# Square sums on TensorE, a new order of need in the first stage, and weights asked for ahead of the queries, in a two-layer diffusion backbone

## The chip, the cores and the metric

The kernel runs on 1 core of one Trainium2 chip. The metric is device time in microseconds (us) for one execution; lower is better. Given is the median of several runs. The engines are named as the profile names them: PE is TensorE (matmul) and PEld its weight load, DVE is VectorE, ACT is ScalarE, POOL is GpSimd, SP is SyncE, whose queue issues nearly all DMA transfers.

## The reference

A backbone of two layers runs over 1280 tokens of width 1024: 256 context tokens and 1024 latent ones. A layer normalizes its input, modulates it by a vector from the conditioning, mixes the tokens and adds the result back through a gate.

```
def rms_norm(x, g):
    y = x * lax.rsqrt(jnp.mean(x * x, axis=-1, keepdims=True) + EPS)
    return y * g
def modulation(cond, w, b):
    return jnp.split(jax.nn.silu(cond) @ w + b, 3, axis=-1)
for i in range(DEPTH):                                  # DEPTH = 2
    sh_l, sc_l, g_l = modulation(c, mod_w[i], mod_b[i])
    sh_c, sc_c, g_c = modulation(c_ctx, mod_w[i], mod_b[i])
    h_lat = rms_norm(x_lat, norm_g[i]) * (1.0 + sc_l) + sh_l
    h_ctx = rms_norm(x_ctx, norm_g[i]) * (1.0 + sc_c) + sh_c
    if i % 2 == 0: y_lat, y_ctx = even_mixer(h_lat, h_ctx, ...)
    else:          y_lat, y_ctx = odd_mixer(h_lat, h_ctx, ...)
    x_lat = x_lat + g_l * y_lat
    if i < DEPTH - 1: x_ctx = x_ctx + g_c * y_ctx
return rms_norm(x_lat, final_g)
```

Layer 0 (even) has two kinds of grouped attention, a global one with rotary and normalized queries and keys, and a banded one with a sink logit. Layer 1 (odd) has a gated convolution over 31 tokens and a neighbourhood attention on the grid. The projections in front of each are one large matmul of `h`.

## The kernel before, in words

The 1280 tokens are kept transposed, with the width on the partitions: 8 tiles of 128 (index `dk`, constant `DK`). Tokens go in three chunks: chunk 0 is the context (256 tokens), chunks 1 and 2 are 512 latent tokens each. All is fp32. A product of full accuracy is made of three matmuls (`mm3`, L344): each operand is split into a high part, rounded by an ACT cast (L325), and a rest, which POOL or DVE gets by subtraction (L328, or L339 in one step with the shift). So `hh`/`hl` are the two parts of a latent chunk's `h`, `hc` both parts of the context's, `wh`/`wl` those of weights.

A norm is made in steps. ACT squares the eight tiles; the squares are added up tile by tile (`acc`); a matmul with `ones` adds over the partitions (`trs`, L262, in `rstd_steps`); DVE scales it (`rbv`, L265); POOL raises it to -1/2 (L247) and three small DVE steps refine that (`nt`, `nt`, `nr`, L248 to L250); a matmul with the identity spreads it over the partitions (`bc`, L273). `make_h` (L330) then multiplies x by the gain and `bc` on DVE (L335, 8 instructions per chunk), and ACT adds the shift. There is also `sum4` (L276), in which four matmuls with 32 columns each add four tiles of squares into four quarters of one PSUM bank (L280). Before the change only the final norm uses it.

The first stage is written out by a string of events, `PLAN`: `p` constants, `0` `1` `2` load a chunk, `n` squares and adds (`norm_x`, L733), `b` `trs` to `bc` (`norm_bc`), `h` `make_h`, `m` a half of the modulation (a GEMV whose 32-column matmuls are `pm`, L183), `w` the first unit's weights. All three chunks go through it before `fill0(0, w0)` is run, which projects the first of four key/value units (`pq`: per block of 128 tokens, 8 x 3 matmuls of 384 columns; the transposes behind it are `trk`) and the first gate blocks (`pg`). Then comes the main loop: attention of one unit, woven with the projection of the next. `load_q` (L617, in `group0`) brings a block of queries from DRAM, over the SP queue.

The order in which each engine gets its instructions is not the order of the code: a scheduler simulates the program and sorts each engine's instructions by its own estimate, with priorities. `issue_after(ins)` pins an instruction behind `ins`, if both are on the same engine.

At the end of layer 0, `final_proj(c)` (L981) adds the output projection into x and makes the squares of layer 1's norm: for chunk 1, one ACT square per tile and seven adds (L1000), alternating between POOL and DVE. In the attention of that stretch, `QL` (L451) carries a running maximum into the scores, `st` are the scores, `ov` the sums over values, `mx` the matmuls for a maximum. In the tail, `final_norm` multiplies the output by `final_g` and `bc` on DVE (L1508) or POOL (L1498), block by block, with pins; the adds of the last block before it are L1440.

Of the kernel before, what the change touches and what calls it, by code (L numbers as in the profile page):

```python
# [10 lines left out]
F32 = mybir.dt.float32  # L11
F32R = mybir.dt.float32r
ALU = mybir.AluOpType
# [59 lines left out]
PLAN = 'p0mmnbwmm1h2nbhnbh'  # L73
MWR = "ABxAVx"
XA = 4
ORDER = (2, 3, 0, 1)
# [11 lines left out]
def tile_kernel(ctx: ExitStack, tc: tile.TileContext, a, out):  # L88
# [164 lines left out]
    last = []  # L253

    def rstd_steps(pool, accs, n, tag, inv=1.0, tr="tr"):
# [4 lines left out]
        for b in range(nb):  # L260
            for k, acc in enumerate(accs):
                last.append(PE.matmul(tr[:, 2 * b : 2 * b + 2], acc[:, b * P : (b + 1) * P], ones, start=(k == 0),  # L262
                                      stop=(k == len(accs) - 1)))
        v = pool.tile([P, 8], F32, tag="rbv", name=nm("rbv"), bufs=2)
        rv = VE.tensor_scalar(v[:, :nb], tr[:, 0 : 2 * nb].rearrange("p (b two) -> p b two", two=2)[:, :, 0],  # L265
                              inv, EPS, op0=ALU.mult, op1=ALU.add)
        r = newton_rsqrt(pool, v[:, :nb], nb, "rb")
# [4 lines left out]
        for b in range(nb):  # L272
            PE.matmul(bc[:, b * P : (b + 1) * P], r[:, b : b + 1].broadcast_to([P, P]), ident, start=True, stop=True)  # L273
# [41 lines left out]
    acts = []  # L315
# [14 lines left out]
    def make_h(l, c, xs, bc, h):  # L330

        cond = 1 if c == 0 else 0
        for dk in range(DK):
            x = xs(dk)
            VE.scalar_tensor_tensor(x, x, gs[l][:, dk, cond : cond + 1], bc, op0=ALU.mult, op1=ALU.mult)  # L335
# [4 lines left out]
            else:  # L340
                SC.activation(x, x, AF.Identity, bias=shift)
                split(x, h[0][:, dk, :], h[1][:, dk, :])

# [11 lines left out]
    def load_w(pool, src, blk, width, bufs, leng="g", dks=range(DK), rb=WPR):  # L355
# [4 lines left out]
        for d2 in sorted({dk // 2 for dk in dks}):  # L360
# [3 lines left out]
            SY.dma_start(raw[:, k], src[blk, d2, :, k])  # L364
# [249 lines left out]
    def group0(u, qb):  # L614
        isb = u >= 2

        def load_q(QH, QL):  # L617
            src = Qd[u][qb].rearrange("(e d) s a t -> d s e (a t)", e=2)
            for dst, s in ((QH[0:64, :], 0), (QH[64:128, :], 0), (QL[0:64, :], 1)):
                SY.dma_start(dst.bitcast(F32).rearrange("d (e c) -> d e c", e=2), src[:, s])  # L620
# [85 lines left out]
    with ExitStack() as p0x:  # L706
# [6 lines left out]
        with tc.tile_pool(name="st0", bufs=1, reuse_waits="tile") as st0:  # L713
# [19 lines left out]
            def norm_x(c):  # L733
                n = CHUNKS[c][1]
                acc = kvp.tile([P, 512], F32, tag="QH", name=nm("acc"), bufs=3)
                for dk in range(DK):
                    if dk == 0:
                        SC.activation(acc[:, :n], xraw[c][0], AF.Square)
                    else:
                        sq = kvp.tile([P, 512], F32, tag="QL", name=nm("sq"), bufs=3)  # L740
                        SC.activation(sq[:, :n], xraw[c][dk], AF.Square)
                        VE.tensor_tensor(acc[:, :n], acc[:, :n], sq[:, :n], op=ALU.add)
                return acc

            def norm_bc(c, acc):
                n = CHUNKS[c][1]
                return run(rstd_steps(st0, [acc], n, "st"))[:, :n]
# [920 lines left out]
```

## Time and profile before

| what | value |
|---|---|
| median of 3 runs | 1542.24 us (1541.05 to 1546.29) |
| profiled execution | 1542.41 us, its span 1540.6 us |
| granted TensorE clock, mean | 0.971 |
| TensorE busy | 95% of the span |
| VectorE, POOL, ScalarE busy | 68%, 51%, 48% |
| DMA | 199.83 MB, mean 130 GB/s |
| chain that ended last, by engine | PE 76%, DVE 12%, DMA 5%, issue 3% |

A row of the timeline has the start, the time, the engine, the line of the kernel, the operation and its tiles (output `<-` inputs), the shape and the count; in brackets stands how long the engine was idle before it, and what released it. A row of windows has the busy time of each engine in a stretch, and at its end the granted TensorE clock (1.00 is full speed), the DMA share and GB/s. Times in a timeline are of matmuls that overlap: how far apart they start says more than how long each takes.

### The profile page before, as it was taken

The numbers are of one execution on the slowest core, as the hardware profiler recorded it, in microseconds if no ns is written. First come the engines' busy times: TensorE is split into PE (matmuls) and PEld (weight loads), VectorE is DVE, ScalarE is ACT, GpSimd is POOL, SyncE is SP. The second block draws the span as 40 slices with busy tenths as digits, with TensorE's granted clock in tenths as the row PEclk, the third lists the DMA queues.
The fourth block names the chain that finished last, engine by engine and source line by source line (L and its number), as shares of the span: only waits on it lengthen the run. The fifth ranks groups of instructions, "written<-read, shape, count | busy, mean of one in ns | idle before, by whom it ended". The sixth has DMA issues, their size and how long they took to land.

```text
span 1540.6 us, 21500 instructions
## 1 busy us (share of the span) xinstructions
PE 1457.2 (95%) x7112; PEld 1171.6 (76%) x7112; DVE 1042.5 (68%) x2106; ACT 746.1 (48%) x1416; POOL 793.3 (51%) x631
## 2 busy tenths in 40 slices
PE   6899999998998999999999889999999999989996
PEld 2776888796896777886776558888887788868875
DVE  2833466479678956556667948999938675567866
ACT  3721434444444455447546665443434455455564
POOL 3440335446355757557646665665533434364664
PEclk7899999999999999999999889999999999999998
DMA  9474315423312236121111112211484677877642
GB/s 367 151 243 145 103 62 175 147 64 93 120 56 71 89 124 225 52 69 53 42 43 58 44 33 79 59 56 41 141 258 143 204 214 225 261 225 235 186 125 109
DMA packets 154168, 199.83 MB, mean 130 GB/s; under 512 B 14717, under 2 KB 95817, under 8 KB 154057
## 3 DMA queue, kind: packets, MB, share of 16 engines
q1 hardware_dynamic: 147392, 186.88, 38.6%
q10 hardware_dynamic: 6664, 11.57, 2.2%
q8 instruction: 56, 0.92, 0.3%
q14 instruction: 56, 0.45, 0.1%
HBM read 148.07 MB, written 49.02 MB: 128 GB/s over the span
## 4 chain that ended last, share of the span: by engine, by line
PE 76%; DVE 12%; DMA 5%; issue 3%; POOL 2%; ACT 2%; SPq 0%; DVEq 0%; POOLq 0%; ACTq 0%
PE p L345 6%; PE p L346 6%; PE p L347 6%; PE ov L473 4%; PE ov L475 4%; PE ov L474 4%; PE po L345 4%; PE po L347 4%; PE po L346 4%; PE st L522 4%; PE st L526 4%; PE pq L345 3%; PE pq L346 3%; PE pq L347 3%; PE pg L345 2%
## 5 line engine op out<-in xcount | busy, mean ns | idle before, releaser
L328 POOL TENSOR_TENSOR pl<-pf,ph 128x512 fp32r<-128x512 f32 (+4 forms) x321 | 395.3, 1243 | 369.2 <-ACT ph L325 305.8
L534 ACT ACTIVATE pf<-st 128x512 f32<-128x512 f32 x284 | 166.3, 597 | 199.3 <-PE st L526 160.8
L328 POOL TENSOR_TENSOR wl<-wr,wh 128x512 fp32r<-128x512 f32 (+2 forms) x131 | 171.0, 1317 | 145.9 <-ACT wh L325 131.5
L325 ACT CAST ph<-pf 128x512 fp32r<-128x512 f32 (+4 forms) x364 | 209.4, 588 | 28.2 <-PE ov L474 17.9
L345 PE MATMUL p<-hh,wh 128*128 128x512 f32 x448 | 176.2, 394 | 3.1 <-DVE spq L1166 1.4
L346 PE MATMUL p<-hl,wh 128*128 128x512 f32 x448 | 174.5, 390 | 0.0
L347 PE MATMUL p<-hh,wl 128*128 128x512 f32 x448 | 173.0, 391 | 0.0
L522 PE MATMUL st<-QH,KAt 128*128 128x512 f32 (+4 forms) x364 | 141.7, 390 | 6.9 <-ACT pf L534 6.0
L473 PE MATMUL ov<-ph,Vt 128*128 128x512 f32 (+4 forms) x364 | 140.8, 387 | 3.8 <-DVE y L683 2.0
L475 PE MATMUL ov<-pl,Vt 128*128 128x512 f32 (+4 forms) x364 | 141.0, 387 | 2.1 <-POOL pl L328 2.0
L474 PE MATMUL ov<-ph,Vt 128*64 128x512 f32 (+4 forms) x364 | 138.9, 382 | 0.0
L526 PE MATMUL st<-QL,KBt 68*128 68x512 f32 (+4 forms) x364 | 136.5, 386 | 0.9 <-issue 0.8
L325 ACT CAST wh<-wr 128x512 fp32r<-128x512 f32 (+2 forms) x134 | 81.0, 612 | 96.3 <-PE p L346 18.7
L1110 DVE SCALAR_TENSOR_TENSOR cps<-U,taps,cps 128x512 f32<-128x512 f32 x184 | 125.9, 749 | 0.7
L345 PEld LDWEIGHTS p<-hh,wh 128*128 128x128 f32 x448 | 84.2, 188 | 21.2 <-ACT wh L325 1.8
L347 PEld LDWEIGHTS p<-hh,wl 128*128 128x128 f32 x448 | 84.1, 188 | 17.5
L346 PEld LDWEIGHTS p<-hl,wh 128*128 128x128 f32 x448 | 84.2, 188 | 16.8 <-issue 0.2
L646 DVE TENSOR_REDUCE mp<-mx 128x1 f32<-128x512 f32 x128 | 85.2, 680 | 17.2 <-PE mx L645 16.3
L345 PE MATMUL pq<-wh,hh 128*128 128x384 f32 x256 | 88.0, 344 | 2.8 <-ACT hh L325 2.8
L967 DVE SCALAR_TENSOR_TENSOR x<-po,modT,x 128x512 f32<-128x512 f32 (+1 forms) x72 | 47.0, 657 | 63.2 <-PE po L347 62.8
L522 PEld LDWEIGHTS st<-QH,KAt 128*128 128x128 f32 x364 | 70.0, 193 | 24.4 <-ACT pf L534 9.1
L475 PEld LDWEIGHTS ov<-pl,Vt 128*128 128x128 f32 x364 | 70.1, 193 | 22.4 <-POOL pl L328 5.0
(283 smaller groups left out, 3473.8 us busy)
## 6 DMA issues: line engine op xcount, KB each, us to landing
mw<-in_mod_w_dram SPq DMA_DIRECT2D x16, 1024.0 KB, 5.5
Q<-qs SPq DMA_DIRECT2D x40, 256.0 KB, 2.2
QH<-Q SPq DMA_DIRECT2D x80, 128.0 KB, 2.7
mw<-in_mod_w_dram SPq DMA_DIRECT2D x16, 512.0 KB, 6.5
wr<-in_od_d_dram SPq DMA_DIRECT2D x32, 256.0 KB, 3.2
wr<-in_ev_qkv_dram SPq DMA_DIRECT2D x16, 384.0 KB, 5.2
KAt<-KD SPq DMA_DIRECT2D x16, 384.0 KB, 6.5
wr<-in_od_wo_dram SPq DMA_DIRECT2D x22, 256.0 KB, 3.4
```

The costliest lines, as they stand in the source:

```text
L325: acts.append(SC.copy(hi, src))
L328: (GP if leng == "g" else VE).tensor_tensor(lo, src, hi.bitcast(F32), op=ALU.subtract)
L345: PE.matmul(o, lh, rh, start=first, stop=False)
L346: PE.matmul(o, lh, rl, start=False, stop=False)
L347: last.append(PE.matmul(o, ll, rh, start=False, stop=end))
L473: PE.matmul(o, V[:, 64:192], ph[:, :n], start=(t == 0), stop=False)
L474: PE.matmul(g.ov[0:64, q0 : q0 + n], V[:, 0:64], ph[:, :n], start=False, stop=False)
L475: PE.matmul(o, V[:, 64:192], pl[:, :n], start=False, stop=(last and g.sink is None))
L522: sts.append(PE.matmul(st[:, :n], KA[:, cs], g.QH[:, q0 : q0 + n], start=True, stop=False))
L526: PE.matmul(st[:, :n], KB[0:68, cs], g.QL[0:68, q0 : q0 + n], start=False, stop=True)
L534: acts.append(SC.activation(pf[:, :n], st[:, :n], AF.Exp, scale=1.0 if g.bias else SCALE))
L1110: VE.scalar_tensor_tensor(pc, uc, w, pc, op0=ALU.mult, op1=ALU.add)
```

## The change

It has five parts.

1. *First stage.* Chunk 1's eight squares are kept, and two `sum4` groups on PE add them into one bank; ACT copies that to `acc`, and the scale 1/32 makes up for the 32 columns. The string has chunk 1's squares and norm ahead of chunk 0's `make_h`. Chunk 2's squares, norm and `make_h` leave the string: the new `start0` runs them at steps 6, 12 and 14 of the first unit's projection, with pins: the squares behind chunk 0's last cast and the copy, the adds behind chunk 1's last x multiply, `trs` behind the last recorded matmul. `BCP` pins two places of the first unit's `pq` (block 1 from dk = 6, block 5 from dk = 1) behind the last recorded `bc`.
2. *Second unit's weights.* They are asked for right behind the first unit's projection, and the first three query loads are pinned behind the last of these loads.
3. *End of layer 0.* `final_proj(1)` adds its squares by two `sum4` groups and one ACT copy in place of seven adds.
4. *Final pins.* In the first of the last blocks, DVE's multiply of tile 1 is pinned behind the last eight adds, and those of later tiles behind the root's third step. In the next block, POOL's multiply is pinned behind a DVE step (before: behind the POOL power).
5. The rest of the program is the same, but the scheduler re-times it.

```diff
-PLAN = 'p0mmnbwmm1h2nbhnbh'
+PLAN = 'p0mmnbwmm1nh2bh'
+S2 = (6, 12, 14)
+BCP = ((1, 6), (5, 1))
...
             def norm_x(c):
                 n = CHUNKS[c][1]
+                if c == 1:
+                    pb = bank("st", nm("pb"))
+                    for q in range(2):
+                        sqs = []
+                        for i in range(4):
...
+                            SC.activation(sq[:, :n], xraw[c][4 * q + i], AF.Square)
+                            sqs.append(sq)
+                        sum4(pb, sqs, n, q)
+                    acc = kvp.tile([P, 512], F32, tag="QH", name=nm("acc"), bufs=3)
+                    acts0.append(SC.copy(acc[:, :n], pb[:, :n]))
+                    return acc
...
-        for _ in fill0(0, w0):
-            pass
+        def start0(w):
+            for k, _ in enumerate(fill0(0, w)):
+                if k == S2[0]:
+                    acc = norm_x(2)
+                if k == S2[1]:
+                    b2 = rstd_steps(ap, [acc], 512, "st", pin=last[-1], vn=("ss", 16, "sr"))
+                    next(b2)
+                if k == S2[2]:
+                    with tc.issue_after(last[-1].ins):
+                        bc = run(b2)
+                    make_h(0, 2, lambda dk: xraw[2][dk], bc, h[2])
+
+        start0(w0)
+        w1 = load_w0("ev_qkv", ORDER[1])
+        firstq += 3 * dmas[-1:]
...
         def load_q(QH, QL):
+            with ExitStack() as cx:
+                if firstq:
+                    cx.enter_context(tc.issue_after(firstq.pop().ins))
...
-                weave(main, n1, fill0(k + 1), NFILL[k], False)
+                weave(main, n1, fill0(k + 1, w1 if k == 0 else None), NFILL[k], False)
...
-                if e < na:
+                if c == 1:
+                    sqs.append(op_.tile([P, 512], F32, tag="sq1" if e % 4 < 3 else "acc1", name=nm("sq1"), bufs=3 if e % 4 < 3 else 1))
+                    SC.activation(sqs[-1], x1[c][:, e, :], AF.Square)
+                    if e == 0:
+                        pb = bank("tr", nm("pb"))
+                    if e % 4 == 3:
+                        sum4(pb, sqs[-4:], n, e // 4)
+                    if e == 7:
+                        accs[c].append(acc1())
+                        SC.copy(accs[c][0], pb)
+                elif e < na:
...
                         if k == 1:
-                            cx.enter_context(tc.issue_after(roots[-1][1].ins))
+                            cx.enter_context(tc.issue_after(roots[-1][2].ins))
...
-                        if k == 0 and e > 1:
-                            pins = adds[-DK:] + ([roots[-2][2]] if e > 3 else [])
+                        if k == 0:
+                            pins = [roots[-2][2]] if e > 1 else adds[-DK:]
```

What it moves is shown at three places. The line numbers of the kernel after are up to some seventy higher; the numbers of tiles differ between the two.

The first place is PE in the first stage, where chunk 0's `pq` end. Before:

```order
L347 MATMUL pq_558<-wh_287,hc_171 128x384
L347 MATMUL pq_588<-wh_287,hc_171 128x384
L262 MATMUL trs_414<-ones,acc_391 128x2 x4
L262 MATMUL trs_483<-ones,acc_460 128x2 x4
L273 MATMUL bc_427<-ident,nr_421 128x128 x4
L345 MATMUL pq_629<-wh_269,hh_172 128x384
```

After (`trs_418` and `bc_431` are chunk 1's; `pq_564` is its first projection):

```order
L353 MATMUL pq_493<-wl_288,hc_171 128x384
L267 MATMUL trs_418<-ones,acc_372 128x2 x4
L354 MATMUL pq_493<-wh_287,hc_171 128x384
L278 MATMUL bc_431<-ident,nr_425 128x128 x4
L352 MATMUL pq_523<-wh_287,hc_171 128x384
L353 MATMUL pq_523<-wl_288,hc_171 128x384
L354 MATMUL pq_523<-wh_287,hc_171 128x384
L352 MATMUL pq_523<-wh_287,hc_171 128x384
L353 MATMUL pq_523<-wl_288,hc_171 128x384
L354 MATMUL pq_523<-wh_287,hc_171 128x384
L352 MATMUL pq_564<-wh_269,hh_172 128x384
```

Chunk 2's sums (`trs_483`) are no longer between chunk 1's sums and its `bc`; one `pq` of chunk 0 stands between them, and six stand behind `bc`. The two new groups of sums stand 21 matmuls and more ahead of this place, on PE after:

```order
L286 MATMUL pb_347<-sq_354,one 32x512
L286 MATMUL pb_347<-sq_348,one 32x512
L286 MATMUL pb_347<-sq_350,one 32x512
L286 MATMUL pb_347<-sq_352,one 32x512
L353 MATMUL pq_523<-wl_276,hc_171 128x384
L354 MATMUL pq_523<-wh_275,hc_171 128x384
L286 MATMUL pb_347<-sq_366,one 32x512
L286 MATMUL pb_347<-sq_360,one 32x512
L286 MATMUL pb_347<-sq_362,one 32x512
L286 MATMUL pb_347<-sq_364,one 32x512
```

Seventeen `pq` follow these rows up to chunk 1's `trs`.

The second place is PE later in the first unit's projection, where a part of the modulation (`pm`) goes. Before:

```order
L183 MATMUL pm_715<-mw_642,csil 32x512
L892 MATMUL trk_826<-ident,pc_628 128x128
L183 MATMUL pm_715<-mw_642,csil 32x512 x3
L183 MATMUL pm_715<-mw_644,csil 32x512 x2
L345 MATMUL pq_836<-wh_269,hh_174 128x384
L183 MATMUL pm_715<-mw_644,csil 32x512
L346 MATMUL pq_836<-wl_270,hh_174 128x384
L183 MATMUL pm_715<-mw_644,csil 32x512
```

After:

```order
L354 MATMUL pq_941<-wh_269,hl_175 128x384
L352 MATMUL pq_941<-wh_269,hh_174 128x384
L185 MATMUL pm_686<-mw_577,csil 32x512 x4
L185 MATMUL pm_686<-mw_579,csil 32x512 x4
```

The eight matmuls of this part stood in five pieces; now they are two whole groups in a row.

The third place is DVE at the end of layer 0. Before (`x_1776` is chunk 1's x, `QL_8450` belongs to an attention block):

```order
L429 TENSOR_REDUCE nmt_8534<-mp_8465 128x4
L248 TENSOR_TENSOR nt_9167<-nr_9166,rbv_9164 128x4
L249 SCALAR_TENSOR_TENSOR nt_9167<-nt_9167,nr_9166 128x4
L250 SCALAR_TENSOR_TENSOR nr_9166<-nt_9167,nr_9166 128x4
L328 TENSOR_TENSOR hc_7129<-y_8633,hc_7129 128x2x128
L328 TENSOR_TENSOR pl_8733<-pf_8734,ph_8732 128x512
L451 TENSOR_TENSOR QL_8450<-trn_8569,k_bd 4x512
L635 TENSOR_REDUCE mp_8639<-mx_8640 128x2
L335 SCALAR_TENSOR_TENSOR x_1776_7151<-x_1776_7151,gs_105,bc_9220 128x512 x8
```

After:

```order
L656 TENSOR_REDUCE mp_8469<-mx_8521 128x1
L656 TENSOR_REDUCE mp_8469<-mx_8535 128x1
L436 TENSOR_REDUCE nmt_8538<-mp_8469 128x4
L341 SCALAR_TENSOR_TENSOR x_1778_7155<-x_1778_7155,gs_105,bc_9228 128x512 x8
L458 TENSOR_TENSOR QL_8454<-trn_8573,k_bd 4x512
L645 TENSOR_REDUCE mp_8643<-mx_8644 128x2
```

The eight x multiplies of chunk 1's `make_h` stood behind this block's `QL`; now they stand ahead of it.

More of the change, by code (lines that the diff above doesn't have):

```diff
@@ L251, in newton_rsqrt, with rstd_steps @@
         return r
-    last = []
-    def rstd_steps(pool, accs, n, tag, inv=1.0, tr="tr"):
+    last, bcm = [], []
+    def rstd_steps(pool, accs, n, tag, inv=1.0, tr="tr", pin=None, vn=("rbv", 8, "rb")):
         nb = n // P
@@ L261, in rstd_steps @@
             for k, acc in enumerate(accs):
-                last.append(PE.matmul(tr[:, 2 * b : 2 * b + 2], acc[:, b * P : (b + 1) * P], ones, start=(k == 0),
-                                      stop=(k == len(accs) - 1)))
-        v = pool.tile([P, 8], F32, tag="rbv", name=nm("rbv"), bufs=2)
+                with ExitStack() as cx:
+                    if pin is not None:
+                        cx.enter_context(tc.issue_after(pin.ins))
+                    last.append(PE.matmul(tr[:, 2 * b : 2 * b + 2], acc[:, b * P : (b + 1) * P], ones, start=(k == 0),
+                                          stop=(k == len(accs) - 1)))
+        v = pool.tile([P, vn[1]], F32, tag=vn[0], name=nm("rbv"), bufs=2)
         rv = VE.tensor_scalar(v[:, :nb], tr[:, 0 : 2 * nb].rearrange("p (b two) -> p b two", two=2)[:, :, 0],
                               inv, EPS, op0=ALU.mult, op1=ALU.add)
-        r = newton_rsqrt(pool, v[:, :nb], nb, "rb")
+        r = newton_rsqrt(pool, v[:, :nb], nb, vn[2])
         roots.append((rv, *newt))
@@ L746, in norm_bc @@
                 n = CHUNKS[c][1]
-                return run(rstd_steps(st0, [acc], n, "st"))[:, :n]
+                return run(rstd_steps(st0, [acc], n, "st", 1.0 / 32.0 if c == 1 else 1.0))[:, :n]
             made = [0]
-            accs, bcs, mh = [], [], [(0, 0), (0, 1), (1, 0), (1, 1)]
+            sums, acts0, accs, bcs, mh = [], [], [], [], [(0, 0), (0, 1), (1, 0), (1, 1)]
             mwp[0] = st0
@@ L768, in tile_kernel @@
                 elif ev == "h":
-                    make_h(0, made[0], lambda dk, c=made[0]: xraw[c][dk], bcs[made[0]], h[made[0]])
+                    xg = make_h(0, made[0], lambda dk, c=made[0]: xraw[c][dk], bcs[made[0]], h[made[0]])
+                    if made[0] == 0:
+                        acts0.append(acts[-1])
+                    if made[0] == 1:
+                        sums.append(xg)
                     made[0] += 1
```

57 lines of the change are left out of this document (39 added, 18 removed).

## The prediction

> **What bounds the kernel now.** The first page and its slices of the span come first: TensorE is the engine that is nearly always busy, and the slices in which it is not are the first, the ones about 5/9 of the way, and the last. So I read three places: the start (to 110 us), the end of layer 0 (840 to 940) and the tail (from 1515).
>
> ```profile
> span 1540.6 us, 21500 instructions
> ...
> PE 1457.2 (95%) x7112; PEld 1171.6 (76%) x7112; DVE 1042.5 (68%) x2106; ACT 746.1 (48%) x1416; POOL 793.3 (51%) x631
> ```
>
> The profiled execution took 1542.41 us, 1.8 more than its span and 0.17 above the median of the three runs, 1542.24; I add to 1542.4. About 0.3%, 4.6 us, is what a measurement of this kernel can tell from no change.
>
> At the start TensorE's timeline shows this (pq is the projection of the first unit, trs the column sums of the squares, bc the broadcast of 1/rms; the last bracket is idle time and its releaser):
>
> ```profile
> 46.91 0.33 PE L347 MATMUL pq<-wh,hc 128*128 128x384 f32 x1
> 47.08 0.33 PE L345 MATMUL pq<-wh,hc 128*128 128x384 f32 x1
> ...
> 47.77 0.95 PE L262 MATMUL trs<-ones,acc 128*128 128x2 f32 x8
> 52.10 1.84 PE L262 MATMUL trs<-ones,acc 128*128 128x2 f32 x8 [3.38 <-DVE nt L249]
> 53.80 2.06 PE L273 MATMUL bc<-ident,nr 128*128 128x128 f32 x8
> 58.61 0.69 PE L345 MATMUL pq<-wh,hh 128*128 128x384 f32 x1 [2.76 <-ACT hh L325]
> ...
> 59.42 0.52 PE L345 MATMUL pq<-wh,hh 128*128 128x384 f32 x1
> 59.74 0.52 PE L346 MATMUL pq<-wl,hh 128*128 128x384 f32 x1
> ```
>
> TensorE runs out of chunk 0's pq at 47.8, does chunk 1's sums, and then stands for 3.38 us in front of chunk 2's sums, which are queued ahead of chunk 1's bc; bc is followed by another 2.76. What those sums wait for is on VectorE and GpSimd:
>
> ```profile
> 51.26 0.69 DVE L742 TENSOR_TENSOR acc<-acc,sq 128x512 f32<-128x512 f32 x1
> ...
> 55.26 0.16 DVE L248 TENSOR_TENSOR nt<-nr,rbv 128x4 f32<-128x4 f32 x1 [1.12 <-POOL nr L247]
> ...
> 55.89 5.36 DVE L335 SCALAR_TENSOR_TENSOR xr<-xr,gs,bc 128x512 f32<-128x512 f32 x8 [0.27 <-PE bc L273]
> ```
> ```profile
> 54.22 1.01 POOL L247 TENSOR_TENSOR nr<-rbv,mhalf 128x4 f32<-128x4 f32 x1 [3.12 <-DVE rbv L265]
> 58.64 3.81 POOL L328 TENSOR_TENSOR hl<-xr,hh 128x512 fp32r<-128x512 f32 x3 [3.41 <-ACT hh L325]
> ```
>
> VectorE adds squares one by one, 0.69 each, for both chunks, up to 51.9. The idle stretches also cost clock: pq starts 0.17 us apart at 47 and 0.32 apart at 59.
>
> **The change, part by part. (1) First chunk-1 projection.** Chunk 1's seven adds leave VectorE; two groups of four narrow matmuls enter TensorE. The same width stands in the modulation's pm, four of which (x8 in the records) run side by side:
>
> ```profile
> 86.45 1.04 PE L183 MATMUL pm<-mw,csil 128*32 128x512 f32 x2
> ...
> 87.69 1.90 PE L183 MATMUL pm<-mw,csil 128*32 128x512 f32 x10
> ...
> 91.25 1.04 PE L183 MATMUL pm<-mw,csil 128*32 128x512 f32 x2
> ...
> 106.10 1.92 PE L183 MATMUL pm<-mw,csil 128*32 128x512 f32 x16
> ```
>
> Two whole groups take 1.92 at 106.10, so one takes about 1.0. Chunk 0 has 26 pq left where the first group stands (about 42.1, counted back from 47.77 at 0.173 with its small waits): 1.0, two pq, 1.0 bring TensorE to 44.5. Then the new order has 17 pq, 2.95, so chunk 1's sums go at 47.4, end at 48.4, and bc is next but for one pq. Between them lie one VectorE step, the power on GpSimd (1.01) and three VectorE steps, all of 0.16: 0.16 + 1.01 + 3 x 0.16 and 0.35 of hops (my estimate, five of 0.07), 2.0; so bc starts at 50.4. It takes 2.06 at half clock (53.80), so 1.03 at full, and ends at 51.5. The first chunk-1 pq came 2.75 after bc's end (55.86 to 58.61); by that, 54.2, and 55.2 at half clock, against 58.61: **4.4 or 3.4 earlier**. Six chunk-0 pq now lie behind bc and cut the second wait to 1.7; the first is 1.9. The ACT copy of the sums (about 0.6) goes between ACT's casts, and its cover is the 17 pq.
>
> Which clock? The longer waits of 1 to 3 us further on show it, and windows give the clock (the figure third from the end):
>
> ```profile
> 745.69 0.50 PE L345 MATMUL po<-hh,wh 128*128 128x512 f32 x1 [1.73 <-ACT hh L325]
> ...
> 1362.91 0.77 PE L1338 MATMUL mx<-KAt,QH 128*128 128x256 f32 x2 [2.26 <-DMA QH<-QD]
> ```
> ```profile
> 745.00:747.00 2.00, 1.31 (x9) 1.23 (x10) 0.06 (x1) 1.97 (x4) 1.29 (x1) 1.00 0.27 93
> 1364.00:1367.00 3.00, 3.00 (x11) 2.40 (x10) 2.92 (x6) 2.20 (x5) 2.21 (x3) 0.65 1.11 277
> ```
>
> A wait of 1.73 left the clock at 1.00. One of 2.26 took it to half for some 2.5 us, and after the one of 3.38 the 2.06 of bc and the 0.32 between pq show half as well. The two new waits are 1.9 and 1.7, with only 2.1 of work between them. I take the first for harmless, being nearest to the 1.73 row, and the second for one that finds the clock halved, since the two together are well over 2.26; both ends are kept for the range.
>
> The Trainium skill, "TensorE: Matmul & The Clock Gate" (Part 1: The HAM clock gate), has the rate halve after an idle window of about 3.4 us. The 2.26 row differs: half rate came earlier here. By the page neither new wait would halve it, and the sum would be the one at full clock below.
>
> **(2) From there to the end of chunk 2's pq** (47.5 us before, 58.61 to 106.1). At full clock the first twelve pq save 12 x (0.32 - 0.173) = 1.8, but then GpSimd's hl (1.27 each by the 58.64 row) runs behind them: about 1.05 back. At half clock both are zero. Chunk 2's sums move in here, 0.95. The modulation's eight matmuls from 86.45 to 92.3 (four stretches in the timeline, the first and the last of 1.04, the longest 1.90, each cut off from the others by pq or trk; together 4.8 to 5.0 of TensorE) become two whole groups, 1.92: 2.9 less. The sums: full clock throughout 4.4 + 1.8 - 1.05 - 0.95 + 2.9 = 7.1; half from bc on 3.4 - 0.95 + 2.9 = 5.3; half from the first chunk-1 pq on 4.4 - 0.95 + 2.9 = 6.3. **Taken: 6.3.** Behind 106 TensorE is the bound, so the gain stays.
>
> Chunk 2's chain is now the late one: its adds stand behind chunk 1's eight x multiplies (5.36). Its bc falls about 70.5 to 71.5, and 20 pq (3.5) are held behind it; its first hh is there 2.75 after bc, at 74.2, its first pq due about 75. The cover is 0.8 us.
>
> **(3) Second unit's weights ahead of the first queries.** SyncE's queue and the first use:
>
> ```profile
> 105.74 1.24 SPq L620 DMA_DIRECT2D QH<-Q  x2
> ```
> ```profile
> 133.19 0.40 PE L633 MATMUL mx<-KAt,QH 128*128 128x256 f32 x2
> ```
>
> The third pair of queries was asked for at 105.7, and all three come no later than about 108 with two weight loads ahead. The first use would be at 133.2 - 6.3 = 127. Nothing is bought and nothing paid; if the queue stood 13 us longer it would be TensorE's loss one for one.
>
> **(4) End of layer 0.** Seven adds on VectorE and GpSimd go, two groups on TensorE and one ACT copy come.
>
> ```profile
> 844.38 0.68 DVE L1000 TENSOR_TENSOR acc<-acc,sq 128x512 f32<-128x512 f32 x1
> ...
> 850.54 0.65 DVE L1000 TENSOR_TENSOR acc<-acc,sq 128x512 f32<-128x512 f32 x1
> ...
> 857.60 1.75 DVE L1000 TENSOR_TENSOR acc<-acc,sq 128x512 f32<-128x512 f32 x1
> ...
> 869.49 0.68 DVE L451 TENSOR_TENSOR QL<-trn,k_bd 4x512 fp32r<-4x512 f32 x1 [0.17 <-PE trn L450]
> 871.07 5.36 DVE L335 SCALAR_TENSOR_TENSOR x<-x,gs,bc 128x512 f32<-128x512 f32 x8 [0.18 <-PE bc L273]
> ```
> ```profile
> 860.55 0.50 PE L522 MATMUL st<-QH,KAt 128*128 128x512 f32 x1 [3.14 <-ACT pf L534]
> ```
> ```profile
> L1000 POOL TENSOR_TENSOR acc<-acc,sq 128x512 f32<-128x512 f32 x6 | 8.2, 1368 | 4.9 <-ACT sq L998 4.9
> ```
> ```profile
> 860.00:880.00 20.00, 17.69 (x68) 12.57 (x68) 18.07 (x33) 12.90 (x25) 11.10 (x9) 0.83 0.02 7
> 880.00:900.00 20.00, 17.41 (x56) 11.54 (x57) 11.65 (x20) 13.65 (x24) 14.67 (x12) 0.74 0.03 7
> ```
>
> TensorE pays about 2.9 (the new order splits the first group in two: three pieces of 0.97). VectorE is rid of 3.1 (the three rows), GpSimd of four at 1.37. VectorE is the busier engine there (18.07 of 20), and TensorE stood 3.14 behind it. But the eight x multiplies, 5.36, now stand ahead of the next attention block's QL instead of behind it. The ends are -3.1 (all of VectorE's share comes back) and +2.9 (none does). **Taken: 0**, as TensorE idles 2.3 to 2.6 of every 20 here, which can take the sums in.
>
> **(5) Layer 1's order** changes where the scheduler re-times it; no row prices it: 0, with 1.5 either way as my estimate.
>
> **(6) Tail.**
>
> ```profile
> 1518.60 1.87 DVE L1508 SCALAR_TENSOR_TENSOR x<-x,fg,bcs 128x512 f32<-128x512 f32 x1 [0.75 <-ACT bcs L1490]
> 1520.39 3.21 DVE L1440 SCALAR_TENSOR_TENSOR x<-po,modT,x 128x256 f32<-128x256 f32 x8
> ...
> 1528.13 0.74 DVE L1508 SCALAR_TENSOR_TENSOR x<-x,fg,bcs 128x512 f32<-128x512 f32 x1
> ...
> 1531.54 0.67 DVE L248 TENSOR_TENSOR nt<-nr,rbv 128x2 f32<-128x2 f32 x1
> ```
> ```profile
> 1520.92 0.39 PE L345 MATMUL po<-od,wh 128*128 128x256 f32 x1 [0.75 <-DVE x L1440]
> ```
> ```profile
> 1531.47 1.41 POOL L1498 TENSOR_TENSOR x<-x,bcs 128x256 f32<-128x256 f32 x2
> ```
>
> The 1.87 multiply ahead of the last block's adds moves behind them: the adds start 1.1 sooner. It returns later as one more multiply of 0.74 between two roots. GpSimd's multiply of 1.41 now stands ahead of the last power, which delays it about 0.6 (my estimate: the 1.41, less what it can start sooner), while nt and its follower (0.67 beside GpSimd's multiply at 1531.47; the same step took 0.16 at 55.26) get shorter by 0.5 each. TensorE, which feeds the adds, waited 0.75 for them, so of the 1.1 that much is on the path: -0.7 + 0.7 + 0.6 - 1.0 = -0.4. The ends are -1.1 and +0.7. **Taken: -0.4.**
>
> Sum: 1542.4 - 6.3 - 0 - 0 - 0 - 0.4 = **1535.7**.
>
> **The rivals.** *First: chunk 2's chain takes the place of the wait removed.* For it: a cover of 0.8 in (2), GpSimd's hl and a VectorE queue of 5.36 ahead of the chain. Against it: SyncE and ACT have nothing new there. If the chain is 1.5 later, TensorE waits about 0.7 at chunk 2's first pq and, with the waits for hl behind it, starts at half clock once more (1.8): 1535.7 + 2.5 = 1538.2. Chance 0.16: no difference.
>
> *Second: the end of layer 0 pays for the sums.* TensorE's 2.9 comes uncovered, since its waits there are for ACT and VectorE steps of the attention that the sums do not shorten: 1535.7 + 2.9 = 1538.6, and 1540.1 with (5)'s 1.5. Chance 0.16: no difference.
>
> *Third, slower: the x multiplies ahead of QL.* At the end of layer 0 the next block's QL, and with it its scores, waits for 5.36 of VectorE. If nothing in TensorE's queue covers that, it is 5.4 lost; the sums' 2.9 come on top, and a stretch at half clock follows (20 us at 0.83 lose 3.4). Together 11.7, less 6.7: 1542.4 + 5.0 = 1547.4. It decides once the uncovered wait passes 6.7 + 4.6 - 2.9 - 3.4 = 5.0. Against it: attention matmuls of the block before are in TensorE's queue at that place. Chance 0.08.
>
> *Fourth: the clock stays whole through both waits.* For it the 1.73 row, against it the 2.26 row: 1542.4 - 7.1 - 0.4 = 1534.9, faster. Chance 0.25. By the page named above this is the outcome.
>
> **How the numbers follow.** The forecast, clock halved at the second wait or at the first (1535.7 to 1536.7), has 0.35. The range goes down to the fourth rival with (4)'s and (6)'s low ends, 1534.9 - 3.1 - 0.7 = 1531.1, taken as 1531; on the high side to both of the first two rivals together with (5)'s 1.5, 1535.7 + 2.5 + 2.9 + 1.5 = 1542.6. It leaves out the third rival. Faster is 0.35 + 0.25 = 0.60, the same 0.16 + 0.16 = 0.32, slower 0.08.
>
> **What would show it.** Right: the first pq<-wh,hh near 54 to 55; no sums of chunk 2 ahead of chunk 1's bc; the last chunk-2 pq near 100; pm in whole groups; the first mx near 127 with no wait for a DMA; in the tail the last block's adds 1 us closer to the end. Wrong: a wait over 1.5 us for hh at chunk 2's first pq, one of 3 us or more for QL near 865, or the lead of 6 us at 110 no longer there at 930.

## The result, and the profile after

The changed kernel takes 1536.87 us (median of 22 runs, 1529.63 to 1542.94) against 1544.28 (22 runs, 1540.57 to 1552.09) for the kernel before: a ratio of 0.995 with a 95% interval of 0.9936 to 0.9964, that is 5.6 to 9.9 us faster. The medians differ by 7.4. 1535.7 was forecast from the one profiled execution of before, 6.7 us less than it. The profiled execution of after spans 1532.5 us, 8.1 less than that of before, and one such difference is not the ratio: the 22 runs of the changed kernel alone lie up to 13 us apart.

TensorE's timeline of the changed kernel answers to the first lines of the prediction (the same columns; lines are those of the changed file):

```profile
46.85 0.95 PE L267 MATMUL trs<-ones,acc 128*128 128x2 f32 x8
...
49.73 1.16 PE L278 MATMUL bc<-ident,nr 128*128 128x128 f32 x8 [1.66 <-DVE nr L252]
...
53.65 0.69 PE L352 MATMUL pq<-wh,hh 128*128 128x384 f32 x1 [0.99 <-ACT hh L331]
54.14 0.52 PE L353 MATMUL pq<-wl,hh 128*128 128x384 f32 x1
54.46 0.52 PE L352 MATMUL pq<-wh,hh 128*128 128x384 f32 x1
...
83.20 1.92 PE L185 MATMUL pm<-mw,csil 128*32 128x512 f32 x16
...
99.00 1.92 PE L185 MATMUL pm<-mw,csil 128*32 128x512 f32 x16
...
126.05 0.40 PE L643 MATMUL mx<-KAt,QH 128*128 128x256 f32 x2
```

The two waits of 3.38 and 2.76 are now 1.66 and 0.99; the first chunk-1 projection is at 53.65 instead of 58.61; the modulation part that stood in four stretches from 86.45 on is one piece of 1.92 at 83.20; chunk 2's projection ends at 99.0 instead of 106.1, and the first attention block's mx starts at 126.05 instead of 133.19. Executions begin their first stage up to 2 us apart (the first trs at 21.96 to 23.98 in the profiles), so from here on I count from the start of chunk 0's sums (the first trs):

```profile
22.82 0.38 PE L262 MATMUL trs<-ones,acc 128*128 128x2 f32 x2 [0.26 <-DVE modT L192]
```
```profile
23.72 0.59 PE L267 MATMUL trs<-ones,acc 128*128 128x2 f32 x2 [0.26 <-DVE modT L194]
```

From there to the first mx it is 133.19 - 22.82 = 110.4 before and 126.05 - 23.72 = 102.3 after. At the end of layer 0, the windows after (the second is the 20 us from the start of bc) and VectorE:

```profile
840.00:860.00 20.00, 20.00 (x94) 13.46 (x92) 15.66 (x30) 10.37 (x20) 10.17 (x8) 1.00 0.27 94
860.50:880.50 20.00, 15.92 (x56) 9.73 (x57) 19.72 (x31) 16.10 (x29) 16.45 (x12) 0.83 0.00 0
```
```profile
861.77 5.36 DVE L341 SCALAR_TENSOR_TENSOR x<-x,gs,bc 128x512 f32<-128x512 f32 x8
867.15 0.68 DVE L458 TENSOR_TENSOR QL<-trn,k_bd 4x512 fp32r<-4x512 f32 x1
```

Before, the 20 us from the start of bc, and ACT ahead of the wait of 3.14 that TensorE had at 860.55:

```profile
870.00:890.00 20.00, 15.65 (x52) 9.46 (x51) 19.61 (x31) 15.26 (x28) 16.40 (x12) 0.79 0.00 0
```
```profile
859.38 0.63 ACT L998 ACTIVATE sq<-x 128x512 f32<-128x512 f32 x1 [2.21 <-DVE acc L1000]
859.92 1.07 ACT L534 ACTIVATE pf<-st 128x512 f32<-128x512 f32 x2
```

ACT stood 2.21 us in front of a square until VectorE's add of 1.75 was done, and the pf that TensorE waited for stood behind that square. With the adds gone this wait is gone, and TensorE is busy for the whole of the first 20 us. Behind bc, with the x multiplies ahead of QL, it is busy for 15.92 where before it was 15.65. (The row of 17.69 in the prediction begins 10 us ahead of bc, so it is not the same stretch.)

### The profile page after: what moved, and what is told of

Read it like the earlier page. It is cut to its first block, busy times and chain, and to the rows that moved or that the text cites. A ratio compares the mean times of both kernels' runs of the same rounds, so it can differ in the third digit from the quotient of the medians.

```text
span 1532.5 us, 21546 instructions
## 1 busy us (share of the span) xinstructions
PE 1454.4 (95%) x7144; PEld 1168.7 (76%) x7144; DVE 1031.3 (67%) x2096; ACT 747.0 (49%) x1418; POOL 786.2 (51%) x627
## 4 chain that ended last, share of the span: by engine, by line
PE 80%; DVE 11%; issue 3%; DMA 3%; POOL 1%; ACT 1%; SPq 0%; DVEq 0%; POOLq 0%; ACTq 0%
PE p L352 6%; PE p L353 6%; PE p L354 6%; PE ov L480 5%; PE ov L482 5%; PE ov L481 4%; PE st L533 4%; PE st L529 4%; PE po L352 4%; PE po L354 4%; PE po L353 4%; PE pq L352 4%; PE pq L353 4%; PE pq L354 4%; PE pg L352 2%
## 5 line engine op out<-in xcount | busy, mean ns | idle before, releaser
L353 PE MATMUL pq<-wl,hh 128*128 128x384 f32 x256 | 87.4, 341 | 0.0
```

The lines of the kernel that those rows point to most:

```text
L353: PE.matmul(o, lh, rl, start=False, stop=False)
```

## The experiments

Each ratio is to the kernel before, with its 95% interval. The runs were made in three groups (e1 to e4, e5 to e8, e9 to e12), each beside its own runs of the kernel before. The last column of the table is the time from the first sums to the first mx, worked out from the profile of each run as above.

| run | ratio | first sums to first mx, us |
|---|---|---|
| before | 1 | 110.4 |
| the change | 0.995 (0.9936 to 0.9964) | 102.3 |
| e1_first_only | 0.9981 (0.9959 to 1.0003) | 110.0 |
| e2_all_but_first | 0.9965 (0.9944 to 0.9986) | 109.9 |
| e3_l0_only | 0.9971 (0.9953 to 0.999) | 110.1 |
| e4_tail_only | 0.9995 (0.9977 to 1.0014) | 110.7 |
| e5_queries_undone | 0.998 (0.9962 to 0.9998) | 110.7 |
| e6_no_l0 | 0.9937 (0.9915 to 0.996) | 102.8 |
| e7_after_again | 0.9934 (0.9909 to 0.9959) | 102.3 |
| e8_ql_first | 0.9946 (0.9925 to 0.9967) | 104.3 |
| e9_mrow_first | 0.9954 (0.9938 to 0.9971) | 102.8 |
| e10_order_only | 0.9983 (0.9967 to 0.9998) | 104.7 |
| e11_filler | 0.9961 (0.9949 to 0.9973) | 103.6 |
| e12_pm_grouped | 0.9926 (0.9902 to 0.9951) | 97.3 |

**The first stage alone (e1_first_only).** The changed kernel with its other parts taken back:

```diff
-        w1 = load_w0("ev_qkv", ORDER[1])
-        firstq += 3 * dmas[-1:]
-                weave(main, n1, fill0(k + 1, w1 if k == 0 else None), NFILL[k], False)
+                weave(main, n1, fill0(k + 1), NFILL[k], False)
```

together with the adds of the end of layer 0 and the final pins as before.

> Only the first stage's part of the change: TensorE sums for chunk 1, the new order of need, chunk 2's norm inside the first unit's projection; the weights of the second unit, the end of layer 0 and the final pins are as before. Theory F (the first stage carries the gain): about 7 us faster than before, ratio 0.9955; the first chunk-1 projection near 53.7, the modulation group behind chunk 2's projection near 99. Theory L (a part of the gain comes from the end of layer 0, where the lead grew from 7.1 at the first attention block to 10.9 at 918 between the two profiles): only 4 to 5 us faster, ratio 0.997.

Neither theory has it. The first chunk-1 projection and the modulation part were early, as forecast, but the first mx came 110.0 after the first sums, as late as before: the stage's gain was there at 99 us and gone at 132. TensorE's timeline shows where:

```profile
97.25 1.92 PE L185 MATMUL pm<-mw,csil 128*32 128x512 f32 x16
...
107.72 1.87 PE L190 MATMUL trm<-msel,mrow 128*128 128x2 f32 x8 [4.24 <-ACT mrow L234]
```

ACT's says why:

```profile
106.36 0.83 ACT L331 CAST wh<-wr 128x768 fp32r<-128x768 f32 x1 [8.16 <-DMA wr<-in_ev_qkv_dram]
107.09 0.58 ACT L234 COPY mrow<-pm 128x512 f32<-128x512 f32 x1
```

ACT stood 8.16 us in front of a cast of the second unit's weights, and the modulation row that TensorE needed stood behind that cast, though the matmuls that the row copies had ended at 99.2.

**Everything but the first stage (e2_all_but_first).** The string, the sums and chunk 2's norm as before:

```diff
-PLAN = 'p0mmnbwmm1nh2bh'
+PLAN = 'p0mmnbwmm1h2nbhnbh'
-BCP = ((1, 6), (5, 1))
+BCP = ()
```

> The first stage as before; the weights ahead of the queries, the sums at the end of layer 0 and the final pins as in the change. Theory F: within 1.5 us of before, ratio 0.999 to 1.001. Theory L: 2.5 to 4 us faster, ratio 0.9975 to 0.998.

The ratio, 0.9965, is 5.4 us less with an interval of 2.2 to 8.6. That is beyond theory L's 0.9975 to 0.998, which the interval holds; theory F's 0.999 to 1.001 it does not hold. Up to the first attention block nothing was won (109.9): the weights ahead of the queries are worth nothing without the first stage.

**The end of layer 0 alone (e3_l0_only)** and **the final pins alone (e4_tail_only).** In both the first stage and the queries are as before; one keeps the two groups of sums in the final projection, the other only the pins:

```diff
-                        if k == 0 and e > 1:
-                            pins = adds[-DK:] + ([roots[-2][2]] if e > 3 else [])
+                        if k == 0:
+                            pins = [roots[-2][2]] if e > 1 else adds[-DK:]
```

> Only the sums at the end of layer 0 differ from before. Theory F: the sums cost TensorE 2.9 and bring VectorE 3.1, which comes to 0, within 1 us; from the last score block before it (about 840) to the wait for the projection's operands (918 before) the stretch is as long as before within 1 us. Theory L: that stretch is 2.5 to 4 us shorter, since the wait of 3.14 for VectorE at 860.5 is gone and its half clock with it; ratio 0.9975 to 0.998.

> Only the final pins differ from before. Theory F: 0.4 us faster, which a ratio does not show (0.9995 to 1); in the trace the stretch from bc of the last block but one (1515.8 before) to the end shortens from 24.8 by 0.4 to 1. Theory T (the tail pays: in the changed kernel's profile the stretch from that bc to the end is 26.1): the stretch is 1 to 1.5 us longer, also with these pins alone.

The sums alone gave 0.9971, 4.5 us with an interval of 1.5 to 7.3, a little beyond theory L's range, which the interval holds. From the transpose for the running maximum (trn) near 824 to chunk 2's sums near 930 the profile takes 107.1 us against 109.4 before. The pins alone gave 0.9995, and the stretch from the bc of the last block but one to the end is 24.84 in its profile against 24.79: neither the 0.4 forecast nor theory T's longer tail. Two parts cancel there: up to the first bc of the last block it takes 12.56 us instead of 13.67, from there to the end 12.30 instead of 11.11.

**The queries undone (e5_queries_undone).** The changed kernel without the early load of the weights (the diff of the first experiment and nothing else).

> The whole change except that the second unit's weights are not asked for ahead of the first queries: the other engines' orders are those of the changed kernel, 13 rows of SyncE's queue differ. Theory W (found in the run with the first stage alone, where ACT stood 8.16 us for wr and TensorE 4.24 us for mrow at 107.7): the same wait comes back, at 105 to 110, with half clock behind it; about 5 us slower than the changed kernel (4.2 and some 1.7 of half clock), ratio to before 0.998 to 0.999; the first attention block's mx at 131 or 132 in place of 126. Theory P (as predicted: costs nothing either way): no such wait, ratio 0.995.

Theory W. SyncE's queue, ACT and TensorE of this run:

```profile
101.41 1.24 SPq L630 DMA_DIRECT2D QH<-Q  x2
102.69 0.60 SPq L630 DMA_DIRECT2D QL<-Q  x1
103.39 0.54 SPq L371 DMA_DIRECT2D wr<-in_ev_qkv_dram  x1
...
104.97 0.63 SPq L371 DMA_DIRECT2D wr<-in_ev_qkv_dram  x1
```
```profile
107.74 0.83 ACT L331 CAST wh<-wr 128x768 fp32r<-128x768 f32 x1 [9.46 <-DMA wr<-in_ev_qkv_dram]
108.47 0.58 ACT L234 COPY mrow<-pm 128x512 f32<-128x512 f32 x1
```
```profile
109.11 1.86 PE L190 MATMUL trm<-msel,mrow 128*128 128x2 f32 x8 [5.54 <-ACT mrow L234]
```

In the changed kernel the same two loads and the same cast read:

```profile
98.59 0.34 SPq L371 DMA_DIRECT2D wr<-in_ev_qkv_dram  x1
...
101.09 0.51 SPq L371 DMA_DIRECT2D wr<-in_ev_qkv_dram  x1
102.17 2.11 SPq L630 DMA_DIRECT2D QH<-Q  x2
```
```profile
102.08 0.83 ACT L331 CAST wh<-wr 128x768 fp32r<-128x768 f32 x1 [2.15 <-DMA wr<-in_ev_qkv_dram]
102.82 0.58 ACT L234 COPY mrow<-pm 128x512 f32<-128x512 f32 x1
```

Counted from the first sums, the third load goes out 6.4 us sooner (74.9 against 81.3), ahead of the query loads that wait for queries still to be written. With the queries in front, TensorE stands 5.54 and goes on at half clock (1.86 for a trm that takes 0.95). 13 rows of one queue are worth 110.7 - 102.3 = 8.4 us here; run beside each other, 0.998 against 0.9934 is 7 us, and each interval reaches 2.8 us or more either way. I had priced these rows at nothing.

**The end of layer 0 as before (e6_no_l0)** and **the changed kernel again (e7_after_again)**, side by side:

```diff
-                if c == 1:
...
-                    if e % 4 == 3:
-                        sum4(pb, sqs[-4:], n, e // 4)
...
-                elif e < na:
+                if e < na:
...
```

> The whole change except that the squares at the end of layer 0 are added on VectorE and GpSimd as before. Theory S (the first stage with the weights ahead is worth 7 to 8, the end of layer 0 about 0): ratio 0.995. Theory L (the end of layer 0 carries 3 to 4.5 of the gain): ratio 0.997 to 0.998, and the stretch from the sums' wait to the projection of chunk 2 is 2 to 4 us longer than in the changed kernel, with TensorE idle for VectorE near 852.

> The changed kernel itself, beside the other three: ratio 0.995 within its interval; in its trace the lead at the first attention block is again 7 to 8 us against before when counted from the first sums, and the rest differs only by stretches at half clock.

0.9937 and 0.9934: on top of the first stage the sums show no gain (0.5 us, and each interval reaches 3.4 us and more either way), as theory S has it. Theory L's wait is in the traces all the same. Without the sums ACT's square stands for VectorE's add again, and TensorE for the pf behind that square:

```profile
850.15 0.63 ACT L1051 ACTIVATE sq<-x 128x512 f32<-128x512 f32 x1 [2.21 <-DVE acc L1053]
```
```profile
851.32 0.80 PE L529 MATMUL st<-QH,KAt 128*128 128x512 f32 x1 [3.13 <-ACT pf L541]
```

TensorE is busy for 16.87 of the 20 us from 840 to 860, where with the sums it is for 20.00. But what that gives does not come through whole. From the transpose near 824 to chunk 2's sums near 930, the profiles give 105.6 to 111.5 with the sums (nine of them) and 109.4 to 112.1 without (before, e1, e4, e6): means of 108.6 and 110.9, 2.3 apart with a scatter as large. In these profiles the difference is one of clock: TensorE is at half clock for 18.2 us of the stretch on average with the sums and for 23.0 without, and less half of that time the means are 99.5 and 99.4 (an estimate, which takes TensorE for busy all that time). 2.3 less is inside the bounds of -3.1 to +2.9, and whether it is 0 or 3 stays open.

**QL ahead of the x multiplies (e8_ql_first).**

```diff
+            with tc.issue_after(qlm[-2].ins) if c == 1 else ExitStack():
                 make_h(1, c, lambda dk: x1[c][:, dk, :], bc[:, :n], h1[c])
```

(qlm holds the instructions that write QL.)

> The changed kernel with chunk 1's eight x multiplies at the end of layer 0 pinned behind the next attention block's QL on VectorE. Theory Q (the third rival's mechanism is there, at a part of its price): QL comes 5 us sooner, TensorE's idle time in the 20 us behind bc shrinks by 1.5 to 3, and the kernel is 1 to 3 us faster than the changed one, ratio to before 0.993 to 0.994. Theory N (what QL gains, the projection of layer 1 loses, since it waits for the same multiplies): no difference, 0.995.

Theory N: 0.9946 beside 0.9934 of the changed kernel, and the stretch that the paragraph above measures took 108.7. QL came 3.6 us behind the start of bc instead of 6.7, but TensorE was busy for 13.89 of the 20 us behind bc, less than the 15.92 of the changed kernel. The third rival's mechanism is there in the order but costs nothing that shows.

**The row ahead of the casts (e9_mrow_first).** Weights behind the queries as in e5, but:

```diff
-            return load_w(w0p, a[src], u, 384, W0B, rb=WRB)
+            with tc.issue_after(mrows[2].ins) if u == ORDER[1] else ExitStack():
+                return load_w(w0p, a[src], u, 384, W0B, rb=WRB)
```

(mrows holds ACT's copies of modulation rows; only ACT's casts are bound by it.)

> As the run with the weights not asked for ahead, but ACT's casts of these weights are pinned behind ACT's copy of the modulation row (mrow) that TensorE waited for. Theory A (what cost 5.5 us was only ACT's queue: the row stood behind a cast whose weights had not landed): the wait of TensorE for mrow is gone, the first attention block comes 102 to 104 us after the first sums, and the kernel is as fast as the changed one, ratio 0.993 to 0.995. Theory D (the late weights themselves hold TensorE up): another wait of 3 to 5 us for wh or for later ACT work takes its place before 140, 108 to 110 us after the first sums, ratio 0.997 to 0.998.

Theory A. ACT and TensorE:

```profile
100.06 0.59 ACT L234 COPY mrow<-pm 128x512 f32<-128x512 f32 x1 [1.11 <-PE pm L185]
100.55 1.57 ACT L331 CAST wh<-wr 128x768 fp32r<-128x768 f32 x2
```
```profile
102.92 0.95 PE L190 MATMUL trm<-msel,mrow 128*128 128x2 f32 x8
```

The two remaining loads go out only at 109.0, some 4.5 to 5.6 us later than in e5, ACT's next cast waits for them up to 117.54, and TensorE does not wait: 102.8 us and 0.9954. So it was not the weights that TensorE needed; ACT took its instructions in order, and one cast too early in that order held up a row. In the kernel before, only two of these casts stood ahead of the row (108.14); the third waited 7.43 us for its weights, up to 117.26, but stood behind the row.

**The order of need without TensorE sums (e10_order_only).** Chunk 1's squares go the way of the other chunks:

```diff
-                if c == 1:
-                    pb = bank("st", nm("pb"))
...
-                    return acc
```

> The whole change, but chunk 1's squares of the first stage are added on VectorE one by one, as before; only the order of need is new. Theory O (the order carries the first stage, the TensorE sums little): the two groups of about 1.0 fall away on TensorE, chunk 1's sums wait for VectorE's last add instead; first chunk-1 projection within 1.5 us of the changed kernel's, the first attention block 102 to 104 us after the first sums, ratio 0.993 to 0.996. Theory E (the adds on VectorE hold it up): chunk 1's bc 3 to 4 us later, 106 to 107 us to the first attention block, ratio 0.996 to 0.997.

Between the two: 104.7 to the first mx, 2.4 behind the changed kernel.

```profile
46.38 1.02 PE L267 MATMUL trs<-ones,acc 128*128 128x2 f32 x8 [0.45 <-DVE acc L759]
49.36 2.07 PE L278 MATMUL bc<-ident,nr 128*128 128x128 f32 x8 [1.95 <-DVE nr L252]
```

TensorE waits 0.45 for VectorE's last add ahead of chunk 1's sums and 1.95 for nr ahead of bc, which then runs at half clock (2.07). So by these profiles most of the stage's 8 us is the order, and some 2 the sums on TensorE. The ratio, 0.9983, is above the ranges of both theories; beside the 0.9954 of e9, measured with it, that is 4.5 us with some 3.5 either way, so the 2.4 lies inside and more than that is not shown.

**Filler in the waits (e11_filler).**

```diff
+            fb = bank("st", nm("fb"))
+            for _ in range(3):
+                with tc.issue_after(last[-1].ins):
+                    fl.append(PE.matmul(fb[:, 0:256], ident, accs[0][:, 0:256], start=True, stop=True))
...
```

and two more ahead of chunk 1's first projection.

> The changed kernel with five matmuls of no use in TensorE's two waits (three of 128x256 between chunk 1's sums and bc, two between the last chunk-0 projection and the first of chunk 1), so that TensorE does not stand idle there. Theory H (half clock from 51 to 58 costs what the prediction's terms say): the clock stays whole, and the first attention block comes 0.8 us sooner after the first sums, 101.5 against 102.3. Theory G (the later parts of h set the pace there, whatever the clock): full clock, but no gain, 102.3. Either way the ratio stays at 0.993 to 0.995.

Theory G. The clock from 54 to 57 was 0.50 in the changed kernel, and it stayed whole here:

```profile
54.00:57.00 3.00, 3.00 (x10) 2.77 (x10) 3.00 (x6) 3.00 (x6) 3.00 (x3) 0.50 0.00 0
```
```profile
54.00:57.00 3.00, 2.54 (x13) 1.95 (x13) 3.00 (x4) 3.00 (x6) 2.81 (x2) 1.00 0.00 0
```

But TensorE now waits around these 3 us instead (2.54 busy), for GpSimd's rests of h (hl), while VectorE and ACT are busy all 3.00:

```profile
53.81 0.45 PE L361 MATMUL pq<-wh,hl 128*128 128x384 f32 x1 [0.41 <-POOL hl L341]
...
56.86 0.44 PE L361 MATMUL pq<-wh,hl 128*128 128x384 f32 x1 [0.46 <-POOL hl L341]
```

No gain: 103.6, and a ratio of 0.9961, a little above the 0.993 to 0.995 that both theories had (the interval begins at 0.9949).

**Modulation in whole groups (e12_pm_grouped).**

```diff
+            with later(-2 * LATE) if dk % 4 and mwp[0] is None else ExitStack():
                 PE.matmul(pb[q : q + 32, :], csil[:, dk, :], w[:, k, :], start=(dk < 4), stop=(dk >= 4))
```

> The changed kernel with three of every four 32-column matmuls of the modulation given a priority, so that they follow their first one: the eight that stood alone between the projections of the gate (1.04 each at 114 to 125) become two groups, and some of the later ones as well. By the term of the prediction (two groups 1.92 where single ones cost 1.04 each): 8 x 1.04 - 1.92 = 6.4 less before the first attention block, 95.9 us after the first sums in place of 102.3, and 3 more by 300 us; in all 6 to 9 us faster than the changed kernel, ratio to before 0.988 to 0.990. Rival (the narrow matmuls stand in waits of TensorE, as fill): the block comes as late as before, ratio 0.993 to 0.995.

```profile
115.18 1.06 PE L186 MATMUL pm<-mw,csil 128*32 128x512 f32 x8
117.62 1.06 PE L186 MATMUL pm<-mw,csil 128*32 128x512 f32 x8
120.36 0.40 PE L644 MATMUL mx<-KAt,QH 128*128 128x256 f32 x2
```

In the changed kernel the first of these matmuls read:

```profile
113.94 1.05 PE L185 MATMUL pm<-mw,csil 128*32 128x512 f32 x2
114.92 0.49 PE L353 MATMUL pg<-hl,gh 128*128 128x512 f32 x1
115.34 1.04 PE L185 MATMUL pm<-mw,csil 128*32 128x512 f32 x2
```

Two pieces of 1.06 stand where eight of 1.04 to 1.05 stood one by one: 97.3 us to the first mx, 5.0 less than the change, where 6.4 was expected. But this execution was at half clock from 25 to 38, as were e8 and the kernel before; the profile of the change was so from 17 to 30. Against e8 it is 7.0 less, and from chunk 1's sums on, which leaves that stretch out, 72.3 us against 79.2: the expected 6.4 came. The ratio, 0.9926, is the lowest of all the kernels, but the 0.988 to 0.990 expected lies outside its interval; against the changed one (0.9934 and 0.995 in its two measurements) its lead of a few us is within the intervals.

## Why the prediction was right, and where its steps failed

**(1) and (2), the first stage: right.** 6.3 was forecast. The profiles give 7.6 to 8.1 by the first mx (the change, e6, e7, e9). In one of the changed kernel's variants (e8) the clock was at half from 25 to 38, as in the profile of before, and there it is 110.4 - 104.3 = 6.1. With the old first stage and the clock whole from 31 to 43 (e2 to e4), the first mx came after 109.9 to 110.7, no sooner than before. So by these profiles that half clock costs the new stage some 2 us (from the first sums to chunk 1's it takes 25.1 and 25.0 in e8 and e12, 22.9 to 23.5 in the other four) and the old one nothing that shows, and the forecast, worked out from a profile that had it, fits that state. The terms held: the first chunk-1 projection 31.9 behind the first sums in e8 where 31.4 to 32.4 was worked out (29.9 in the profile of after), sums to bc 2.88 where 3.0 was worked out, bc to the first hh as before, first projection to the end of chunk 2 45.35 where 47.5 - 2.0 was worked out, pm in one piece.

The clock term was of no use. I weighed 6.3 against 7.1 by when the clock falls; it fell in this profile at 51 and in another of the same kernel (e7) at 54, and not at all there in e8, which has the same first stage, and from chunk 1's sums to the first mx each took 79.2 to 79.4. At whole clock TensorE waits for GpSimd's hl instead, as e11 shows; the 1.8 that I took for the whole clock is paid back in full, not only 1.05 of it. So the fourth rival's clock came in e8 and e11 and brought nothing. That half clock would hold at the first chunk-1 projection or soon behind it was right for these two and did not matter. The half clock behind the wait of 2.26 lasted 3.4 us by the clock record, not the 2.5 that I read from a window. The Trainium skill, "TensorE: Matmul & The Clock Gate" (Part 1: The HAM clock gate), which made the fourth rival, has the rate halve after an idle window of about 3.4 us; in the profile of after it was half behind a wait of 1.66, in e8 the same wait left it whole.

**(3), the weights ahead of the queries: wrong.** "Nothing is bought and nothing paid." I looked at who waits for the queries that are moved back, which was right (the first mx never waited), and not at who waits for the weights that are moved forward. The new first stage was the condition: in the order that the scheduler makes with it, ACT's third cast stands ahead of the row, where before it stood behind it, and TensorE comes to the row sooner. Without those rows of SyncE's queue the first stage is worth nothing at 132 us (e1, e5), with them 8; or the row is put ahead of the casts (e9). The sum came out only because the change held both: a term priced at nothing was what let the 6.3 of (2) through, and that was luck.

**(4), the end of layer 0: taken as 0, still open.** Alone it measured 4.5 faster (1.5 to 7.3; the bound was 3.1), on top of the rest 0.5 with a wide interval. The parts do not add up: this 4.5 and the 7 to 8 of the first stage with the rows of the queue are more than the 7.4 of the whole. The intervals are wide, and why is not shown. The wait that goes is one behind ACT's order, as in (3), not one of TensorE for VectorE itself. The x multiplies ahead of QL cost nothing that shows (e8).

**(5) and (6).** Layer 1 shows no difference that the profiles repeat: the stretch of its attention (trn at 1210 to 1486) takes 272 to 279, whatever the kernel. In the tail the -0.4 did not come. The adds began sooner, as forecast (3.40 behind the bc of the block before instead of 4.58), but the last root came late:

```profile
1521.37 1.94 POOL L1565 TENSOR_TENSOR x<-x,bcs 128x256 f32<-128x256 f32 x2 [2.05 <-ACT bcs L1557]
1523.27 0.69 POOL L249 TENSOR_TENSOR nr<-rbv,mhalf 128x2 f32<-128x2 f32 x1
```
```profile
1521.96 0.15 DVE L270 TENSOR_SCALAR rbv<-trs 128x2 f32<-128x2 f32 x1
...
1523.99 0.16 DVE L250 TENSOR_TENSOR nt<-nr,rbv 128x2 f32<-128x2 f32 x1 [1.10 <-POOL nr L249]
```

The power is delayed by 1.1 (it starts 1.31 behind the start of its rbv, before 0.23) instead of the 0.6 that I took. The short nt and its follower give 1.0 back and the one more multiply costs 0.7, both as worked out, and behind the last bc 0.5 more goes (7.9 to the end instead of 7.45), for which I had no term. So from the last block's first bc to the end it takes 12.3 in all eleven profiles with the pins and 11.1 in the three without. What the sooner adds win ahead of that differs from profile to profile: from the bc of the block before to the end it is 24.8 in e4 and 26.1 in the changed kernel, against 24.8 before. The last block's adds were to stand 1 us closer to the end; they start 22.8 us from it instead of 20.2.

**The rivals.** The first did not come: chunk 2's bc was at 71.3 and its pq followed without a wait over 1 us. The second and the third did not show. What came was a fifth one that I had not listed, a queue on ACT, and the change already held its cure.

## What to carry to other kernels

When a stage gets faster, ask of every engine what stands next in its order and when its data lands: here a cast that had stood behind the row stood ahead of it in the new order, and its weights landed late. Of a load that is moved forward, look at who waits behind its consumer, not only at the transfers that are moved back. And take a stage out alone: here two parts that are worth nothing apart, the first stage and 13 rows of a DMA queue, are worth 8 us together.

## What the runs showed of the hardware

Four 32-column matmuls in a row on different quarters took 1.06 together, and 1.04 to 1.05 each when another matmul stood between them (e12, and the rows of the changed kernel beside it). The half clock came in whole steps: in the traces' clock records of all fourteen profiles its stretches are 3.4, 6.8, 10.2, 13.7 or 17.1 us, multiples of 3.41 (but for the one that the end cuts off), and the same wait of 1.66 was followed by one in some executions and not in others. Total time at half clock was 66 to 93 us in the span of each. Runs of one kernel go with it: of the 22 of the changed kernel the shortest, 1529.63 us, had a mean clock of 0.980 and the longest, 1542.94, one of 0.967, and over all 22 the squared correlation of time and clock is 0.66.
